# First mixer: GpSimd keeps fills and first differences, its other work goes to VectorE; 16-row triangles are inverted as 8-row blocks

## The chip, the cores and the metric

The kernel runs on one core of one Trainium2 chip. The metric is the device time of one execution in microseconds (us); the kernel before takes 2576.1 us (median of 3 runs, 2573.64 to 2580.8). In the profile PE is TensorE, PEld its weight loads, DVE is VectorE, ACT is ScalarE, POOL is GpSimd and SP the queue that issues DMAs.

## What is computed

Two decoder layers on 256 tokens of width 2048, all in float32. The first layer's mixer is RWKV-7, the second's differential attention; each is followed by a gated MLP with a short convolution, and by layer norms. The change is in the first mixer alone, whose core is a recurrence over time per head (32 heads of 64 columns):

```python
def step(S, inp):
    r_t, w_t, k_t, v_t, a_t, b_t = inp
    sa = einsum('bhij,bhj->bhi', S, a_t)
    S = S * w_t[:, :, None, :] + sa[..., None] * b_t[:, :, None, :] + v_t[..., None] * k_t[:, :, None, :]
    y = einsum('bhij,bhj->bhi', S, r_t)
    return S, y
# around it
xx = token_shift(x) - x
xr, xw, xk, xv, xa, xg = (x + xx * mu[i] for i in range(6))
r, k, v = xr @ w_rkv[0], xk @ w_rkv[1], xv @ w_rkv[2]      # and three narrow pairs for decay, a and the gate
y = group_norm(wkv7_scan(r, decay, k, v, -kk, kk * a)) + bonus
return (y * g) @ w_o
```

## The kernel before

Every weight matrix is streamed from memory in chunks of 128 x 512. `chunk` (L199 to L214) splits each 128 x 256 piece into `hi` (ScalarE, L210) and `lo` = raw - hi (L213), and `mm3` multiplies with both parts. L213 runs on VectorE, except for every `pool_every`-th piece (PACE `pool0=3` in the opening products, `pool=4` in the pipeline) and the first chunk of each opening product, which run on GpSimd. TensorE needs `hi` and `lo` of a piece before it can multiply with it.

The mixer goes through three stages. First (0 to about 150 us) the input is mixed with its shifted copy six ways (L773, then split by L191 and L192 into two parts `S`, `S1r`) beside the products for v and for the narrow pairs; the first differences `xx` are L770. Then (to about 200) the first products for r and k. Then (200 to 645) a pipeline over 8 groups of 4 heads. One step of the pipeline runs four generators beside each other, interleaved by the numbers in PACE: `chain` and `outputs` of group i (the recurrence in chunks of 64 tokens, then norm, gate and bonus), `lanes` of group i+1, `front` of group i+2 and `products` of group i+3. The last steps run `early` products with the output weights in place of the products. What the generators issue is put in one fixed order per engine, and each engine runs its list strictly in that order.

`front` (L1064) makes the scaled factors `KB` and `AR` and the 64 x 64 coupling matrices `M` (L1145), and stores M to memory (`d1`, L1153). `lanes` (L1180) inverts the unit triangular part of each M. It loads the 16 x 16 diagonal blocks back from memory (`Ml`, L1191), solves all of them row by row on VectorE (a product L1209 and a reduction L1211 for each of rows 1 to 15, over 8 right-hand columns per lane), stores the result (`d2`, L1215) and loads it as 32 x 32 blocks (`W`, L1220). Blocks of 16 are then joined to 32 (transpose L1227, 32 x 16 products L1233 and L1240) and 32 to 64 (transpose L1245, products L1251 and L1260). `W` is copied back into M (L1266 area, engines named by PACE `wc`).

On GpSimd the mixer has, per group: Lx = L - sw (L1107), the copy pc (L1114), kk times a (L1122), half of KB (L1130), r times k (L1159), fills of Ml and Tl (L1192 to L1196), KB times pc (L1198), one of the four copies of W (L1049 from `wc`), bonus times gate (L1382), and the output sum (L1388).

Of the kernel before, what the change touches and what calls it, by code (L numbers as in the profile page):

```python
# [33 lines left out]
PACE = dict(chain=37.24, front=19.56, lanes=19.55, products=40.92, pool=4, pool0=3, chain0=0, front0=0,  # L34
            lanes0=0, early0=0, products0=0, wc='PVVA', ek='AA', ez='VA', ec='AVAA', ey='V', el='V', w0=(3, 4,
# [924 lines left out]
class Groups:  # L960
# [114 lines left out]
    def front(self, g):  # L1075
# [31 lines left out]
        nc.gpsimd.tensor_tensor(out=Lx, in0=L, in1=sw, op=ALU.subtract)  # L1107
# [14 lines left out]
        nc.gpsimd.tensor_tensor(out=a, in0=kk, in1=a, op=ALU.mult)  # L1122
# [36 lines left out]
        nc.gpsimd.tensor_tensor(out=r, in0=r, in1=k, op=ALU.mult)  # L1159
# [18 lines left out]
    def lanes(self, g):  # L1178
# [15 lines left out]
        for q in range(2):
            r = slice(64 * q, 64 * q + 64)
            nc.gpsimd.memset(Tl[r].rearrange("p a b -> p (a b)")[:, 8 * q:8 * q + 7 * 17 + 1:17], 1.0)  # L1196

        nc.gpsimd.tensor_tensor(out=KB.rearrange("p c a s -> p c (a s)"), in0=KB.rearrange("p c a s -> p c (a s)"),  # L1198
# [166 lines left out]
    def outputs(self, g):  # L1365
# [98 lines left out]
```

## Time and profile before

| what | us |
|---|---|
| median of 3 runs | 2576.1 |
| the profiled execution, whole | 2568.52 |
| its span, first to last instruction | 2566.5 |
| TensorE busy in the span | 2468.5 |
| VectorE busy | 2053.8 |
| ScalarE busy | 1645.2 |
| GpSimd busy | 390.7 |

Busy shares are averages over stages. A matmul's record runs from its start to a modelled end, so that TensorE can look busy while it waits behind a piece that is not there yet. In the rows below a line number is that of the kernel before; `x` is the number of instructions, and behind the bar stand the busy time, the mean ns of one, and the idle time of the engine before them.

### The profile page before, as it was taken

How to read it: one execution, taken by the hardware profiler on the slowest of the kernel's cores; microseconds unless marked ns; L12 is line 12 of the kernel's file. 1: busy time of each engine (PE TensorE's matmuls, PEld its weight loads, DVE VectorE, ACT ScalarE, POOL GpSimd, SP SyncE). 2: the span in 40 equal slices, each digit the busy share in tenths (PEclk: the TensorE clock that was granted, in tenths of full speed). 3: DMA queues.
4: the chain of work that ended last, by engine and by line, in shares of the span. 5: the costliest groups of instructions: out<-in, count | busy, mean ns of one | idle time of the engine just before them, and what ended most of it. 6: DMA issues, size and time to landing. Idle time of an engine off the chain costs nothing.

```text
span 2566.5 us, 54810 instructions
## 1 busy us (share of the span) xinstructions
PE 2468.5 (96%) x17598; PEld 2171.5 (85%) x17598; DVE 2053.8 (80%) x5100; ACT 1645.2 (64%) x4318; POOL 390.7 (15%) x456
## 2 busy tenths in 40 slices
PE   7999989899899999999999999999999999999996
PEld 6888778767788888888889899998888888888886
DVE  8977888887897777777777877779997777777776
ACT  5765555644576666666566766666676666666664
POOL 4343344332400000000111200003300000000111
PEclk9999999999999999999999999999999999999998
DMA  6544334344466555556766555556465555566664
GB/s 191 175 129 116 102 104 108 99 121 124 125 187 192 190 190 190 190 189 184 225 190 183 156 171 171 171 167 196 145 199 188 188 188 188 188 186 185 189 190 127
DMA packets 285186, 429.63 MB, mean 167 GB/s; under 512 B 69081, under 2 KB 91617, under 8 KB 284897
## 3 DMA queue, kind: packets, MB, share of 16 engines
q1 hardware_dynamic: 284896, 426.14, 55.0%
q8 instruction: 137, 2.24, 0.4%
q14 instruction: 153, 1.25, 0.2%
HBM read 421.03 MB, written 6.57 MB: 167 GB/s over the span
## 4 chain that ended last, share of the span: by engine, by line
PE 74%; DVE 4%; ACT 1%; issue 1%; DMA 1%; POOL 0%; ACTq 0%; DVEq 0%; SPq 0%; POOLq 0%
PE psd L225 42%; PE psd L226 21%; PE psd L293 1%; PE psd L291 1%; PE psd L292 1%; DVE lo L213 1%; PE psd L897 1%; PE psd L896 1%; PE psd L898 1%; PE lnst L345 1%; PE psd L221 1%; PE psd L223 1%; PE psd L222 1%; DMA raw<-in_rw_o 0%; PE pss L656 0%
## 5 line engine op out<-in xcount | busy, mean ns | idle before, releaser
L210 ACT CAST hi<-raw 128x256 fp32r<-128x256 f32 (+1 forms) x3128 | 1231.1, 405 | 676.5 <-PE psd L225 461.2
L213 DVE TENSOR_TENSOR lo<-raw,hi 128x256 fp32r<-128x256 f32 (+1 forms) x2984 | 1287.5, 442 | 404.4 <-ACT hi L210 369.4
L225 PE MATMUL psd<-S,hi 128*128 128x512 f32 x3004 | 1056.7, 396 | 0.4 <-ACT hi L210 0.4
L226 PE MATMUL psd<-S,lo 128*128 128x256 f32 x3004 | 842.2, 280 | 4.4 <-DVE lo L213 3.8
L225 PEld LDWEIGHTS psd<-S,hi 128*128 128x128 f32 x3004 | 566.0, 188 | 132.5 <-ACT hi L210 1.2
L226 PEld LDWEIGHTS psd<-S,lo 128*128 128x128 f32 x3004 | 565.8, 188 | 5.9 <-DVE lo L213 4.5
L225 PE MATMUL psd<-hs,hi 128*128 128x512 f32 x1290 | 451.4, 394 | 0.1
L226 PE MATMUL psd<-hs,lo 128*128 128x256 f32 x1290 | 361.5, 280 | 0.0
L225 PEld LDWEIGHTS psd<-hs,hi 128*128 128x128 f32 x1290 | 241.8, 187 | 56.5 <-ACT hi L210 1.0
L226 PEld LDWEIGHTS psd<-hs,lo 128*128 128x128 f32 x1290 | 243.1, 188 | 0.4 <-DVE lo L213 0.3
L363 POOL COPY ln_acc<-X 128x256 f32<-128x256 f32 x4 | 2.1, 528 | 1230.9 <-DVE X L397 1230.9
L213 POOL TENSOR_TENSOR lo<-raw,hi 128x256 fp32r<-128x256 f32 x144 | 130.4, 913 | 301.2 <-ACT hi L210 244.1
L223 PE MATMUL psd<-S,lo 128*128 128x256 f32 x480 | 140.6, 293 | 13.8 <-DVE lo L213 8.4
L221 PE MATMUL psd<-S,hi 128*128 128x256 f32 x480 | 141.6, 295 | 0.9 <-ACT hi L210 0.5
L222 PE MATMUL psd<-S,hi 128*128 128x256 f32 x480 | 141.4, 295 | 0.0
L223 PEld LDWEIGHTS psd<-S,lo 128*128 128x128 f32 x480 | 92.8, 193 | 22.3 <-DVE lo L213 12.8
L225 PE MATMUL psd<-S1r,hi 128*128 128x512 f32 x276 | 109.9, 427 | 1.4 <-ACT o_rs L1049 0.7
L370 POOL TENSOR_TENSOR ln_acc<-ln_acc,X 128x256 f32<-128x256 f32 x49 | 40.9, 834 | 402.4 <-DVE X L409 389.1
L221 PEld LDWEIGHTS psd<-S,hi 128*128 128x128 f32 x480 | 92.5, 193 | 5.7 <-ACT hi L210 1.5
L222 PEld LDWEIGHTS psd<-S,hi 128*128 128x128 f32 x480 | 92.8, 193 | 2.9 <-issue 2.7
L221 PE MATMUL psd<-S1r,hi 128*128 128x256 f32 x284 | 87.2, 307 | 1.4 <-ACT S1r L191 0.9
L897 PE MATMUL psd<-S,lo 128*128 128x258 f32 x256 | 75.4, 295 | 10.1 <-DVE lo L213 10.1
(297 smaller groups left out, 3823.5 us busy)
## 6 DMA issues: line engine op xcount, KB each, us to landing
raw<-in_ff_up SPq DMA_DIRECT2D x676, 256.0 KB, 3.4
raw<-in_ff_down SPq DMA_DIRECT2D x320, 256.0 KB, 3.0
raw<-in_rkv SPq DMA_DIRECT2D x192, 256.0 KB, 3.5
raw<-in_da_qk SPq DMA_DIRECT2D x122, 256.0 KB, 3.4
raw<-in_da_v SPq DMA_DIRECT2D x64, 256.0 KB, 3.1
raw<-in_da_o SPq DMA_DIRECT2D x64, 256.0 KB, 3.5
raw<-in_rw_o SPq DMA_DIRECT2D x50, 256.0 KB, 3.5
raw<-in_ff_down SPq DMA_DIRECT2D x32, 192.0 KB, 2.7
```

The source lines that it names most:

```text
L210: nc.scalar.copy(out=hi[:, :s * P], in_=r)
L213: eng.tensor_tensor(out=lo[:, :s * P], in0=r, in1=hi[:, :s * P].bitcast(F32), op=ALU.subtract)
L221: nc.tensor.matmul(ps[:, :T], lhsT=hi, rhs=xs[:, :T], start=first, stop=False)
L222: nc.tensor.matmul(ps[:, :T], lhsT=hi, rhs=xs[:, T:], start=False, stop=False)
L223: nc.tensor.matmul(ps[:, :T], lhsT=lo, rhs=xs[:, :T], start=False, stop=last)
L225: nc.tensor.matmul(ps, lhsT=hi, rhs=xs, start=first, stop=False)
L226: nc.tensor.matmul(ps[:, T:], lhsT=lo, rhs=xs[:, :T], start=False, stop=last)
L291: nc.tensor.matmul(o, lhsT=xh, rhs=hi, start=k == 0 and b == 0, stop=False)
L292: nc.tensor.matmul(o, lhsT=xh, rhs=lo, start=False, stop=False)
L293: nc.tensor.matmul(o, lhsT=xl, rhs=hi, start=False, stop=k == KT - 1 and b == T // P - 1)
L370: nc.gpsimd.tensor_tensor(out=self.ln_acc[:, hs], in0=self.ln_acc[:, hs], in1=t, op=ALU.add)
L897: nc.tensor.matmul(ps[:, 2:4 + T], lhsT=lo[:, w], rhs=x[:, 2:4 + T], start=False, stop=False)
```

## The change

All lo parts of the pipeline and of the opening products go to VectorE (`pool=0`, `pool0=0`; the first chunk of each opening product stays on GpSimd), and so do the elementwise products and differences of `front`, `lanes` and `outputs`. The GpSimd copy of W goes to ScalarE (`wc='AVVA'`). GpSimd keeps the first differences, fills, the copy pc, and what other stages give it. The triangular solve stops at 8 x 8 blocks: twice as many blocks as before, spread over all 128 lanes, rows 1 to 7, each product and reduction only as wide as the row needs. A new step joins 8 to 16 with a transpose, 32 small products per group, a masked copy into the new tile Z8, and 32 more products. Z2 takes the buffer T1 that tt, T0, T1 and T2 use, one after the other.

```diff
-PACE = dict(chain=37.24, front=19.56, lanes=19.55, products=40.92, pool=4, pool0=3, chain0=0, front0=0,
-            lanes0=0, early0=0, products0=0, wc='PVVA', ek='AA', ez='VA', ec='AVAA', ey='V', el='V', w0=(3, 4,
+PACE = dict(chain=37.24, front=19.56, lanes=19.55, products=40.92, pool=0, pool0=0, chain0=0, front0=0,
+            lanes0=0, early0=0, products0=0, wc='AVVA', ek='AA', ez='VA', ec='AVAA', ey='V', el='V', w0=(3, 4,
...
-        nc.gpsimd.tensor_tensor(out=Lx, in0=L, in1=sw, op=ALU.subtract)
+        nc.vector.tensor_tensor(out=Lx, in0=L, in1=sw, op=ALU.subtract)
...
-        for q in range(2):
-            nc.sync.dma_start(out=self.dram(d2, 0, ((DBL, 64), (C, 8), (1, 16)), at=8 * C * q),
-                              in_=Tl[64 * q:64 * q + 64])
+        nc.sync.dma_start(out=self.dram(d2, 0, ((DBL // 2, P), (C, 8), (1, 8))), in_=Tl)
...
-        for i in range(1, 16):
-            nc.vector.tensor_tensor(out=tt[:, :, :i + 1], in0=Tl[:, :, :i + 1],
-                                    in1=Ml[:, 0:i + 1, i].unsqueeze(1).broadcast_to([P, 8, i + 1]), op=ALU.mult)
-            nc.vector.tensor_reduce(out=Tl[:, :, i], in_=tt[:, :, :i + 1], axis=AX.X, op=ALU.add)
+        for i in range(1, 8):
+            nc.vector.tensor_tensor(out=tt[:, :i, :i], in0=Tl[:, :i, :i],
+                                    in1=Ml[:, 0:i, i].unsqueeze(1).broadcast_to([P, i, i]), op=ALU.mult)
+            nc.vector.tensor_reduce(out=Tl[:, :i, i], in_=tt[:, :i, :i], axis=AX.X, op=ALU.add)
             if i % 3 == 0:
                 yield
...
+        T0 = g1.tile([P, 8, 32], F32, name="T1")
+        nc.vector.transpose(out=T0.rearrange("p u t -> p (u t)"), in_=W1.rearrange("p u t -> p (u t)"))
+        T0v, W1v = (x.rearrange("p u (b k i) -> p u b k i", b=2, k=2) for x in (T0, W1))
+        ps = self.pst()
+        pv = ps[:, :P].rearrange("p (u b i) -> p u b i", b=2, i=8)
+        for u in range(8):
+            for q, r in enumerate(rows):
+                be = 32 * (q % 2)
+                nc.tensor.matmul(pv[r, u], lhsT=N[q][r, u, be:be + 32], rhs=T0v[r, u, :, 0, :], start=True, stop=True)
+        nc.vector.tensor_tensor(out=self.Z8[:, :, :, 0, :], in0=pv,
+                                in1=t.x("m8", 16).rearrange("p (b i) -> p b i", b=2).unsqueeze(1).broadcast_to([P, 8, 2, 8]),
+                                op=ALU.mult)
+        yield
...
+        for u in range(8):
+            for r in rows:
+                nc.tensor.matmul(pv[r, u], lhsT=self.Z8[r, u].rearrange("p b k i -> p (b k i)"), rhs=W1v[r, u, :, 1, :],
+                                 start=True, stop=True)
+        nc.scalar.copy(out=W1v[:, :, :, 1, :], in_=pv)
+        yield
...
-        Z2 = g1.tile([P, 8, 32], F32, name="Z2")
+        Z2 = g1.tile([P, 8, 32], F32, name="T1")
```

Six more instructions change from `nc.gpsimd` to `nc.vector` in the same way: kk times a, half of KB, r times k, KB times pc, bonus times gate and the output sum.

GpSimd's list for one group, in the middle of the pipeline (`lo` is a weight part, `Tl` the tile of the solve). Before:

```order
L1388 TENSOR_TENSOR X<-o_y,bon 128x512
L1107 TENSOR_TENSOR Lx<-L,wa 128x512
L213 TENSOR_TENSOR lo<-raw,hi 128x256
L1114 COPY pc<-eL 128x8
L213 TENSOR_TENSOR lo<-raw,hi 128x256
L1122 TENSOR_TENSOR wa<-kk,wa 128x512
L1130 TENSOR_TENSOR KB<-wa 128x2x2x64 x2
L213 TENSOR_TENSOR lo<-raw,hi 128x256
L1159 TENSOR_TENSOR r<-r,k 128x512
L213 TENSOR_TENSOR lo<-raw,hi 128x256 x2
```

Now, from the opening stage to the first group:

```order
L216 TENSOR_TENSOR lo<-raw,hi 128x256
L773 TENSOR_TENSOR xx<-xz 128x256 x5
L1201 MEMSET Tl 128x64
L1202 MEMSET Tl 128x8
L989 MEMSET UV 128x1024
L994 COPY Z<-cst 32x8x16 x4
L1000 COPY Z_2562<-cst 32x8x8 x8
L1124 COPY pc<-eL 128x8
```

From there on the copy pc and the two fills of Tl are all that stands there for a group; the rest has left this list.

VectorE's list where the solve begins, behind the last join of the group before (`T` is the work tile, `bon` the bonus). Before:

```order
L1254 COPY Z_5198<-pss 32x256
L1209 TENSOR_TENSOR T_5279<-Tl,Ml 128x8x2
L1211 TENSOR_REDUCE Tl<-T_5279 128x8
L1209 TENSOR_TENSOR T_5279<-Tl,Ml 128x8x3
L1211 TENSOR_REDUCE Tl<-T_5279 128x8
L1209 TENSOR_TENSOR T_5279<-Tl,Ml 128x8x4
L1211 TENSOR_REDUCE Tl<-T_5279 128x8
```

Now:

```order
L1280 COPY T_5357<-pss 32x256
L216 TENSOR_TENSOR lo<-raw,hi 128x256
L1115 SCALAR_TENSOR_TENSOR L<-ext,wa 128x256 x2
L1215 TENSOR_TENSOR T_5438<-Tl,Ml 128x1
L1117 TENSOR_TENSOR Lx<-L,wa 128x512
L1217 TENSOR_REDUCE Tl<-T_5438 128x1
L1175 TENSOR_TENSOR bon<-pss,X 128x512
L1215 TENSOR_TENSOR T_5438<-Tl,Ml 128x2x2
L1293 COPY M<-pss 32x8x32
```

The products and reductions are shorter, other work stands between them, and the first product now stands behind the scan and a lo part.

VectorE's list at the joins (`W` is the loaded block, `Z_2562` the tile Z8). Before:

```order
L213 TENSOR_TENSOR lo<-raw,hi 128x256
L1377 SCALAR_TENSOR_TENSOR o_y<-yps,par,o_rs 128x256 x2
L1227 STREAM_TRANSPOSE T_5110<-W_4495 128x256
L1145 TENSOR_TENSOR M<-pss,ext 128x2x256 x2
L213 TENSOR_TENSOR lo<-raw,hi 128x256
```

Now:

```order
L1231 STREAM_TRANSPOSE T_5876<-W_5439 128x256
L216 TENSOR_TENSOR lo<-raw,hi 128x256
L1239 TENSOR_TENSOR Z_2562<-pss,ext 128x16x8
L216 TENSOR_TENSOR lo<-raw,hi 128x256
L1403 SCALAR_TENSOR_TENSOR o_y<-yps,par,o_rs 128x256 x2
L1408 TENSOR_TENSOR bon<-bon,o_rs 128x512
L1155 TENSOR_TENSOR M<-pss,ext 128x2x256 x2
```

The new masked copy waits for TensorE's 32 products of the new join, and only one lo part stands between it and the transpose that feeds them.

## Rows read from the trace of the kernel before

**Rows 1.** The page, part 1: busy us of each engine, share of the span, instructions
```profile
PE 2468.5 (96%) x17598; PEld 2171.5 (85%) x17598; DVE 2053.8 (80%) x5100; ACT 1645.2 (64%) x4318; POOL 390.7 (15%) x456
```

**Rows 2.** Stretches: length, busy us and instructions by engine, clock, DMA share, GB/s
```profile
37.00:150.00 113.00, 104.53 (x804) 98.96 (x803) 111.99 (x252) 79.97 (x232) 43.00 (x48) 1.00 0.57 173
200.00:645.00 445.00, 411.50 (x5016) 339.16 (x5015) 371.07 (x914) 249.88 (x607) 154.92 (x177) 0.95 0.42 111
```

**Rows 3.** The same columns, the two stretches of one group
```profile
351.00:383.00 32.00, 28.14 (x346) 23.61 (x346) 30.58 (x79) 20.15 (x50) 14.17 (x13) 0.95 0.29 89
383.00:402.00 19.00, 18.52 (x286) 16.29 (x282) 12.68 (x28) 9.72 (x23) 6.82 (x9) 1.00 0.59 129
```

**Rows 4.** Groups by shape, GpSimd, 37 to 150: busy, mean ns, idle before
```profile
L213 POOL TENSOR_TENSOR lo<-raw,hi 128x256 fp32r<-128x256 f32 x48 | 43.5, 921 | 70.6 <-ACT hi L210 55.0 <-PE psd L223 9.8 <-PE psd L222 4.1
```

**Rows 5.** Groups by shape, VectorE, 37 to 150
```profile
L773 DVE SCALAR_TENSOR_TENSOR mx<-xx,par,xz 128x256 f32<-128x256 f32 x74 | 44.7, 630 | 0.1
L213 DVE TENSOR_TENSOR lo<-raw,hi 128x256 fp32r<-128x256 f32 x95 | 43.2, 479 | 0.1
L192 DVE TENSOR_TENSOR S1r<-mx,S1r 128x256 fp32r<-128x256 f32 x62 | 28.6, 475 | 0.0
```

**Rows 6.** Groups by shape, VectorE, 770 to 1000, where GpSimd does nothing
```profile
L213 DVE TENSOR_TENSOR lo<-raw,hi 128x256 fp32r<-128x256 f32 x331 | 140.1, 424 | 46.1 <-ACT hi L210 42.3 <-PE psd L225 0.4
L526 DVE SCALAR_TENSOR_TENSOR gc<-gp,cpar,gc 128x256 f32<-128x256 f32 x41 | 19.6, 478 | 0.0
```

**Rows 7.** Timeline of VectorE: start, us, line, tiles, count
```profile
365.36 0.74 DVE L213 TENSOR_TENSOR lo<-raw,hi 128x256 fp32r<-128x256 f32 x2
...
370.43 2.38 DVE L1129 TENSOR_TENSOR KB<-k,wa 128x256 f32<-128x256 f32 x2
```

**Rows 8.** Timeline of GpSimd, same stretch
```profile
366.58 3.64 POOL L213 TENSOR_TENSOR lo<-raw,hi 128x256 fp32r<-128x256 f32 x1
```

**Rows 9.** Groups by shape, GpSimd, 351 to 383
```profile
L213 POOL TENSOR_TENSOR lo<-raw,hi 128x256 fp32r<-128x256 f32 x4 | 6.0, 1505 | 8.9 <-ACT hi L210 5.5 <-PE us L1339 3.3
L1130 POOL TENSOR_TENSOR KB<-wa 128x256 f32<-128x256 f32 x2 | 1.7, 860 | 0.1
L1122 POOL TENSOR_TENSOR wa<-kk,wa 128x512 f32<-128x512 f32 x1 | 1.5, 1476 | 0.0
...
L1107 POOL TENSOR_TENSOR Lx<-L,wa 128x512 f32<-128x512 f32 x1 | 1.3, 1269 | 1.8 <-DVE L L1105 1.8
```

**Rows 10.** Groups by shape, VectorE, 351 to 402
```profile
L213 DVE TENSOR_TENSOR lo<-raw,hi 128x256 fp32r<-128x256 f32 x24 | 10.6, 454 | 3.4 <-ACT hi L210 3.0
...
L1129 DVE TENSOR_TENSOR KB<-k,wa 128x256 f32<-128x256 f32 x2 | 2.4, 1232 | 0.0
...
L322 DVE SCALAR_TENSOR_TENSOR Lx<-Lx,o_y 128x512 f32<-128x512 f32 x1 | 1.1, 1111 | 0.0
...
L1209 DVE TENSOR_TENSOR T<-Tl,Ml 128x16 f32<-128x16 f32 x1 | 0.9, 885 | 0.0
...
L322 DVE SCALAR_TENSOR_TENSOR eL<-eL,t 128x512 f32<-128x512 f32 x1 | 0.7, 670 | 0.0
...
L1209 DVE TENSOR_TENSOR T<-Tl,Ml 128x24 f32<-128x24 f32 x1 | 0.2, 185 | 0.0
...
L1211 DVE TENSOR_REDUCE Tl<-T 128x8 f32<-128x16 f32 x1 | 0.2, 172 | 0.0
```

**Rows 11.** Groups by line, VectorE, 0 to 760: the triangular inversion
```profile
L1209 DVE TENSOR_TENSOR T<-Tl,Ml 128x16 f32<-128x16 f32 (+14 forms) x120 | 42.0, 350 | 3.9 <-POOL Ml L1192 1.7
...
L1211 DVE TENSOR_REDUCE Tl<-T 128x8 f32<-128x16 f32 (+14 forms) x120 | 27.1, 226 | 2.5
```

**Rows 12.** Groups by shape, TensorE, 0 to 760
```profile
L1233 PE MATMUL pss<-T,M 32*32 32x16 f32 x512 | 5.8, 180 | 0.3 <-DVE R L1049 0.3
```

**Rows 13.** DMA issues, 0 to 760: count, KB each, median us to landing
```profile
W<-d SPq DMA_DIRECT2D x32, 32.0 KB, 2.1
d<-Tl SPq DMA_DIRECT2D x16, 32.0 KB, 3.2
```

More of the change, by code (lines that the diff above doesn't have):

```diff
@@ L80, in _const_layout @@
     base = n
-    for name, w in (("bd1", P), ("cent", P), ("mask", P), ("reset", T)):
+    for name, w in (("bd1", P), ("cent", P), ("mask", P), ("reset", T), ("m8", 16)):
         at[name] = n
@@ L109, in _constants @@
     put("mask", np.concatenate([s < t, s <= t], 1).astype(np.float32))
+    m8 = np.ones((P, 16), np.float32)
+    m8[np.arange(P) % 32 >= 24, :8] = 0
+    put("m8", m8)
     reset = np.ones((P, T), np.float32)
@@ L991, in open @@
             nc.gpsimd.tensor_copy(out=self.Z[r, :, 16:], in_=t.cst[r, o:o + 16].unsqueeze(1).broadcast_to([32, 8, 16]))
+        self.Z8 = fx.tile([P, 8, 2, 2, 8], F32, name="Z8")
+        for q in range(4):
+            r = slice(32 * q, 32 * q + 32)
+            for b in range(2):
+                o = CCOL["ident"] + 32 * q + 16 * b + 8
+                nc.gpsimd.tensor_copy(out=self.Z8[r, :, b, 1, :],
+                                      in_=t.cst[r, o:o + 8].unsqueeze(1).broadcast_to([32, 8, 8]))
         self.d2 = d2p.tile([P, DBL * 64 // P], F32, name="d2")
@@ L1120, in front @@
                                     op0=ALU.subtract, op1=ALU.mult)
-        nc.gpsimd.tensor_tensor(out=a, in0=kk, in1=a, op=ALU.mult)
+        nc.vector.tensor_tensor(out=a, in0=kk, in1=a, op=ALU.mult)
         nc.vector.scalar_tensor_tensor(out=k, in0=t1, scalar=1.0, in1=k, op0=ALU.add, op1=ALU.mult)
@@ L1129, in front @@
             nc.vector.tensor_tensor(out=self.half(KB[:, :, par, :], par), in0=k_, in1=e_, op=ALU.mult)
-            nc.gpsimd.tensor_tensor(out=self.half(KB[:, :, 1 - par, :], par), in0=a_, in1=e_, op=ALU.mult)
+            nc.vector.tensor_tensor(out=self.half(KB[:, :, 1 - par, :], par), in0=a_, in1=e_, op=ALU.mult)
         nc.vector.scalar_tensor_tensor(out=AR[:, :, 0, :], in0=c3, scalar=-1.0, in1=_ch(_fl(Lx)), op0=ALU.mult,
@@ L1157, in front @@
             yield from self.gates(g + 1)
-        nc.gpsimd.tensor_tensor(out=r, in0=r, in1=k, op=ALU.mult)
+        nc.vector.tensor_tensor(out=r, in0=r, in1=k, op=ALU.mult)
         for jj, j in js:
@@ L1183, in lanes @@
         KBT = s["KBT"] = self.g2.tile([P, GT * NC, P], F32, name="KBT")
-        Ml = g1.tile([P, 16, 16], F32, name="Ml")
-        Tl = g1.tile([P, 8, 16], F32, name="Tl")
+        Ml = g1.tile([P, 8, 8], F32, name="Ml")
+        Tl = g1.tile([P, 8, 8], F32, name="Tl")
         tt = g1.tile([P, 8, 32], F32, name="T1")
@@ L1188, in lanes @@
         Z = self.Z
-        for q in range(2):
-            nc.sync.dma_start(out=Ml[64 * q:64 * q + 64], in_=self.dram(d1, 0, ((DBL, 64), (C, 16), (1, 16))))
-        nc.gpsimd.memset(Ml.rearrange("p a b -> p (a b)")[:, 0:256:17], 1.0)
+        nc.sync.dma_start(out=Ml, in_=self.dram(d1, 0, ((DBL // 2, P), (C, 8), (1, 8))))
         nc.gpsimd.memset(Tl, 0.0)
[L1194 to L1198, printed above, removed]
+        nc.gpsimd.memset(Tl.rearrange("p a b -> p (a b)")[:, 0:64:9], 1.0)
+        nc.vector.tensor_tensor(out=KB.rearrange("p c a s -> p c (a s)"), in0=KB.rearrange("p c a s -> p c (a s)"),
                                 in1=pc.rearrange("p j c o -> p (j c) o").broadcast_to([P, GT * NC, 2 * C]),
@@ L1381, in outputs @@
         nc.tensor.matmul(ps, lhsT=t.x("bd1"), rhs=_fl(y2), start=True, stop=True)
-        nc.gpsimd.tensor_tensor(out=bon, in0=bon, in1=rs, op=ALU.mult)
+        nc.vector.tensor_tensor(out=bon, in0=bon, in1=rs, op=ALU.mult)
         nc.vector.tensor_scalar(out=_fl(y2), in0=ps, scalar1=1.0 / 64, scalar2=GN_EPS, op0=ALU.mult, op1=ALU.add)
@@ L1387, in outputs @@
         nc.vector.tensor_tensor(out=y, in0=y, in1=rs, op=ALU.mult)
-        nc.gpsimd.tensor_tensor(out=self.V[:, j0:j0 + GT, :], in0=y, in1=bon, op=ALU.add)
+        nc.vector.tensor_tensor(out=self.V[:, j0:j0 + GT, :], in0=y, in1=bon, op=ALU.add)
         if g >= NG - 3:
```

3 lines of the change are left out of this document (2 added, 1 removed).

## Prediction, written before the change was run

> **What bounds the kernel now.** I read the page's busy shares first, then the stretches, then groups of instructions by shape, and last the timelines of VectorE and GpSimd beside each other. Over the whole span TensorE is busy 96% and GpSimd 15% [rows 1], which says nothing about the change, since the change is in the first 650 us. By stretch, two places have another limit than TensorE. From 37 to 150 us VectorE is busy 111.99 of 113 us [rows 2], with TensorE at 104.53. In the pipeline (200 to 645) VectorE has 371.07 of 445 us, but not evenly: one group takes 51 us, of which VectorE is busy in 30.58 of the first 32 and in 12.68 of the next 19, while TensorE has 28.14 and 18.52 [rows 3]. So the first part of a group goes at VectorE's speed and the second, at 97%, at TensorE's. The group behind it has the same two parts. ScalarE is at 20.15 and 9.72 and sets nothing.
>
> **What GpSimd costs VectorE.** A lo part takes VectorE 424 ns on average where GpSimd does nothing [rows 6], 479 from 37 to 150 [rows 5], and 454 within a group [rows 10]. Two products for KB took 2.38 us [rows 7], 1232 ns each [rows 10], while GpSimd worked on its own half; a lo part of the same shape and input count is 424. GpSimd pays too: one of its lo parts lasted 3.64 us behind VectorE's list [rows 8], against a mean of 921 in [rows 4]. The two engines get in each other's way when both read from SBUF.
>
> Sum for 37 to 150, from [rows 5] less the undisturbed 478 and 424 of [rows 6]: 74 x (630 - 478) = 11.2, 95 x (479 - 424) = 5.2, 62 x (475 - 424) = 3.2, in all 19.6 us that VectorE gets back, if no work of GpSimd is left there (the first differences end before 37 us). What comes in: the 48 lo parts [rows 4]. Two lo parts back to back take 0.74 us [rows 7], so one more costs 0.74 - 0.42 = 0.32, taken as 0.34: 16.3 us. Net -3.3; I take -3. Ends: -8.5 (TensorE's idle time there, 113 - 104.5, all gone) and +3 (the 48 parts at their full 424 ns, 20.4 us, with a seventh of the disturbance staying).
>
> **One group of the pipeline, first part (32 us).** Disturbance that goes, from [rows 10]: lo parts 24 x (454 - 424) = 0.7; KB 2 x (1232 - 424) = 1.6; the second Lx step 1111 against 670 for its twin eL, 0.4; the first product of the solve 885 against 185 for the next larger one, 0.7. Sum 3.4 us.
>
> The solve: 42.0 + 27.1 = 69.1 us over 8 groups [rows 11], 8.6 per group. The seven products and reductions that replace it are as wide as 1 to 49 elements; I price each pair as the smallest of the old ones, 185 + 172 ns [rows 10], so 2.5 us. By the line's means (350 and 226) it would be 4.0. Saved 6.1; 4.6 at the other end.
>
> What VectorE takes over in this part: four 512-wide instructions (Lx and kk times a in [rows 9], and two of the same shape, the output sum and r times k), at the 670 ns of an undisturbed 512-wide one [rows 10] 2.7 us; two products for KB at 0.42, 0.8; four lo parts [rows 9] at 0.34, 1.4. Sum 4.9.
>
> Net -3.4 - 6.1 + 4.9 = -4.6 of 32 us. TensorE is busy 28.14 us of it; if all of that were work, only 3.9 could be gained. I take 3.9. Part of what counts as busy there may be records that wait in TensorE's queue, so 3.9 is no hard floor.
>
> **Second part (19 us).** VectorE gets the bonus product (0.67), KB times pc (twice as wide, 1.34), four lo parts (1.4), a transpose and the masked copy: 4 us and some onto 12.68, which fits under 19. TensorE gets two more rounds of small products like L1233, whose 512 records take 5.8 us over 8 groups [rows 12]: 0.72 each, 1.45 per group. Since TensorE sets this part, that is paid: +1.45. The copy of W that ScalarE takes over lies under its idle half. SP issues one load and one store of the blocks per group where it issued two of each; no gain is counted for it. The output sum of a group gets shorter on VectorE, which only the last group can feel, under 1 us, counted at nothing.
>
> **An added wait.** Three instructions on VectorE now stop its list: the first product of the solve waits for TensorE to be done with the shared buffer T1, the first transpose for the loaded W, the masked copy for TensorE's new products. Behind them are lo parts, and TensorE waits for those. Store and load of the blocks take 3.2 and 2.1 us [rows 13]. In the new list about a dozen instructions (lo parts, two M, r times k) stand between last reduction and first transpose, some 5 us, and VectorE has 6.3 us idle in that part. So I cost the stops at nothing; other end 4.5 us per group (2 for the load, 1.5 for the new products behind a transpose, 1 for T1).
>
> **Sum.** Per group -3.9 + 1.45 = -2.45, times 8 = -19.6; with the -3 of the opening, -22.6. The profiled execution took 2568.5 us (span 2566.5, 2.0 around it), so 2545.9, and by the ratio of the median to it (2576.1 / 2568.5) **2553.5 us**, 0.9% less.
>
> **A rule weighed.** The rows on KB and lo parts show mutual delay by amounts between 30 and 800 ns. The Trainium skill, "SBUF — State Buffer", section "Who interferes with whom", says that a VectorE instruction with two SBUF inputs and a GpSimd instruction that reads SBUF exclude each other, the later one standing still for the whole of the other. By it each GpSimd product would cost VectorE up to its whole length; the trace agrees where KB took 1232 ns, and not in the 24 lo parts. What that makes of the time is the last rival.
>
> **Rivals.**
> *TensorE takes it back.* The 28.14 us of TensorE in the first part are work, its own round trips in the recurrence set the pace, and the part gives only the 1.45 that the new products cost. Then -3 is left: 2573. For it: TensorE is at 88% there. Against: VectorE is idle under 1.5 us of 32.
> *The stops decide (slower).* The three stops hold VectorE's list for 4.5 us per group in the part that TensorE sets, and the lo parts behind them come late. Then -3.9 + 1.45 + 4.5 = +2.05, times 8 = +16.4, less 3: +13.4, 2589. It decides from 2.45 us per group on. For it: only one lo part stands between the new transpose and the masked copy. Against: the list moves the same kinds of stops that are there now, and VectorE has 6.3 us free there.
> *More than the sum.* GpSimd's 14.17 busy us in the first part [rows 3] cost VectorE most of their length, in copies and pieces I have not priced, and TensorE's 28.14 us are largely waiting. Then the part loses 8 instead of 3.9: (-8 + 1.45) x 8 = -52, and -8.5 in the opening: 2515. Against: the lo parts of [rows 10], 24 of them, lose 30 ns on average, not 700.
>
> **Chances and range.** Forecast 0.67 (own range 2532 to 2568), TensorE takes it back 0.13, stops 0.12, more than the sum 0.08. About 0.3%, 8 us, is what a measurement of this kernel can tell from no change. Faster by more: 0.67 + 0.08 = 0.75; within: 0.13; slower: 0.12. The 80% range leaves out most of the stops and the lower half of the last rival: 2522 to 2580. The low end also holds a group at -4.6 with the opening at -8.5.
>
> **What would show it.** Right: from 37 to 150 lo parts at about 424 ns on VectorE, the stretch a few us shorter; the period of a group down from 51 to about 48.5; the solve near 2.5 us per group; GpSimd under 10 us in the pipeline. Wrong: VectorE waiting at the masked copy or the first transpose by more than 2 us per group; TensorE's waits for lo parts longer than before; the period unchanged with VectorE idle in the first part, which would say that the recurrence's round trips set it.

## The result: faster, and the profile after

The changed kernel takes 2540.2 us (median of 4 runs, 2539.45 to 2543.21), the kernel before on the same chip 2576.8 (4 runs, 2573.64 to 2580.8): ratio 0.9859, 95% interval 0.9838 to 0.988. The forecast was 2553.5, its 80% range 2522 to 2580. The profiled execution has a span of 2537.5 us against 2566.5, which is 29.0 less.

The page's first part: busy us of each engine, share of the span, instructions. It answers to [rows 1].

```profile
PE 2461.7 (97%) x18622; PEld 2170.2 (86%) x18622; DVE 2030.6 (80%) x5192; ACT 1648.8 (65%) x4334; POOL 172.0 (7%) x236
```

GpSimd has lost more than half of its time. TensorE's busy time is hardly less, over a shorter span. Next, two stretches of the changed kernel (length, busy us and instructions by engine, clock, DMA share, GB/s), against [rows 2]:

```profile
37.00:150.00 113.00, 108.88 (x853) 104.54 (x852) 111.17 (x316) 85.21 (x246) 0.27 (x2) 1.00 0.59 176
200.00:645.00 445.00, 423.19 (x6112) 352.18 (x6113) 371.30 (x972) 264.88 (x655) 12.91 (x34) 0.98 0.42 113
```

VectorE is as busy from 37 to 150 us as before, with 316 instructions in place of 252. From 200 to 645 it has the same 371 us, while TensorE went from 411.50 to 423.19 and its granted clock from 0.95 to 0.98. One group, with the columns of [rows 3]:

```profile
329.00:359.00 30.00, 28.89 (x378) 24.29 (x378) 28.39 (x80) 21.84 (x52) 0.68 (x3) 1.00 0.33 89
359.00:377.00 18.00, 17.91 (x382) 16.01 (x382) 13.04 (x30) 8.89 (x24) 0.00 (x0) 1.00 0.59 140
```

The two parts are 30 and 18 us long where they were 32 and 19, and the clock in the first is 1.00 where it was 0.95. Groups of VectorE's instructions by shape (busy us, mean ns | idle before), first from 37 to 150 us against [rows 5], then in the group from 329 to 377 against [rows 10]:

```profile
L216 DVE TENSOR_TENSOR lo<-raw,hi 128x256 fp32r<-128x256 f32 x153 | 58.3, 416 | 1.0 <-ACT hi L213 0.9
L776 DVE SCALAR_TENSOR_TENSOR mx<-xx,par,xz 128x256 f32<-128x256 f32 x77 | 35.1, 477 | 0.0
L195 DVE TENSOR_TENSOR S1r<-mx,S1r 128x256 fp32r<-128x256 f32 x62 | 25.3, 417 | 0.3
```

```profile
L216 DVE TENSOR_TENSOR lo<-raw,hi 128x256 fp32r<-128x256 f32 x33 | 13.3, 419 | 4.3 <-ACT hi L213 3.9 <-PE us L1365 0.3
...
L1139 DVE TENSOR_TENSOR KB<-k,wa 128x256 f32<-128x256 f32 x2 | 0.8, 418 | 0.0
```

These durations are now within 8 ns of those of [rows 6]. The triangles, by line, 0 to 760 us, against [rows 11]; and TensorE's two added rounds, against [rows 12]:

```profile
L1215 DVE TENSOR_TENSOR T<-Tl,Ml 128x1 f32<-128x1 f32 (+6 forms) x56 | 10.6, 190 | 0.7
...
L1217 DVE TENSOR_REDUCE Tl<-T 128x1 f32<-128x1 f32 (+6 forms) x56 | 9.5, 170 | 0.9
```

```profile
L1247 PE MATMUL pss<-W,Z 32*32 32x16 f32 x512 | 6.2, 180 | 1.1 <-DVE M L1155 0.9
...
L1238 PE MATMUL pss<-T,M 32*32 32x16 f32 x512 | 5.8, 180 | 0.1
```

So the solve went from 69.1 to 20.1 us in all, and the added rounds take 12.0 us.

To see where the 29 us came from I take four marks in both traces: the first copy of r out of PSUM (the opening ends there), the first output o_y that VectorE writes, the fifth, and the end.

| stretch | before | after | difference |
|---|---|---|---|
| start to first r | 156.3 | 149.3 | -7.0 |
| first r to first o_y (the pipeline fills) | 131.1 | 121.4 | -9.8 |
| first to fifth o_y (four periods) | 205.3 | 192.6 | -12.7 |
| fifth o_y to the end | 2073.8 | 2074.3 | +0.5 |

The period of a steady group is 51.3 us before and 48.15 after. What I had not weighed shows in the clock column (the share of full speed that TensorE was granted) of three stretches, first of the kernel before, then of the changed one:

```profile
150.00:280.00 130.00, 119.91 (x1112) 106.83 (x1114) 98.65 (x226) 73.19 (x175) 50.90 (x60) 0.91 0.42 115
280.00:480.00 200.00, 182.62 (x2469) 156.37 (x2465) 173.80 (x416) 119.05 (x283) 79.45 (x87) 0.97 0.39 102
480.00:650.00 170.00, 161.05 (x1809) 123.28 (x1810) 136.38 (x352) 86.62 (x223) 46.86 (x57) 0.94 0.43 119
```

```profile
150.00:280.00 130.00, 123.25 (x1534) 109.88 (x1535) 102.88 (x260) 76.67 (x185) 5.39 (x20) 0.99 0.48 128
280.00:480.00 200.00, 192.61 (x3174) 164.91 (x3172) 174.11 (x450) 131.53 (x314) 2.63 (x12) 1.00 0.40 104
480.00:650.00 170.00, 157.51 (x1822) 123.10 (x1820) 137.68 (x366) 91.07 (x238) 12.26 (x22) 0.97 0.42 120
```

The trace's own records of the granted clock put TensorE at 1.2 instead of 2.4 GHz for 58.0 us of the time from 150 to 650 us before, and for 13.7 us after.

### The profile page after: what moved, and what is told of

The parts are those of the page before. It is cut to its first block, busy times and chain, and to the rows that moved or that the text cites. A ratio compares the mean times of both kernels' runs of the same rounds, so it can differ in the third digit from the quotient of the medians.

```text
span 2537.5 us, 56569 instructions
## 1 busy us (share of the span) xinstructions
PE 2461.7 (97%) x18622; PEld 2170.2 (86%) x18622; DVE 2030.6 (80%) x5192; ACT 1648.8 (65%) x4334; POOL 172.0 (7%) x236
## 4 chain that ended last, share of the span: by engine, by line
PE 81%; DVE 3%; ACT 1%; DMA 1%; issue 1%; SPq 0%; POOL 0%; ACTq 0%; DVEq 0%; POOLq 0%
PE psd L228 43%; PE psd L229 22%; PE psd L224 2%; PE psd L225 2%; PE psd L226 2%; PE psd L296 1%; PE psd L295 1%; PE psd L294 1%; PE psd L900 1%; PE psd L899 1%; PE psd L901 1%; DVE lo L216 1%; DMA raw<-in_rw_o 1%; PE lnst L348 1%; PE pss L1152 0%
## 5 line engine op out<-in xcount | busy, mean ns | idle before, releaser
L216 DVE TENSOR_TENSOR lo<-raw,hi 128x256 fp32r<-128x256 f32 (+1 forms) x3124 | 1308.3, 430 | 418.9 <-ACT hi L213 375.9
L224 PE MATMUL psd<-S,hi 128*128 128x256 f32 x480 | 138.5, 289 | 1.6 <-ACT hi L213 1.4
L225 PE MATMUL psd<-S,hi 128*128 128x256 f32 x480 | 137.6, 287 | 0.0
L228 PE MATMUL psd<-S1a,hi 128*128 128x512 f32 x240 | 84.9, 398 | 0.0
L229 PE MATMUL psd<-S1r,lo 128*128 128x256 f32 x276 | 80.8, 293 | 1.5 <-DVE lo L216 1.5
```

Of the source, the lines that this page charges most:

```text
L216: eng.tensor_tensor(out=lo[:, :s * P], in0=r, in1=hi[:, :s * P].bitcast(F32), op=ALU.subtract)
L224: nc.tensor.matmul(ps[:, :T], lhsT=hi, rhs=xs[:, :T], start=first, stop=False)
L225: nc.tensor.matmul(ps[:, :T], lhsT=hi, rhs=xs[:, T:], start=False, stop=False)
L228: nc.tensor.matmul(ps, lhsT=hi, rhs=xs, start=first, stop=False)
L229: nc.tensor.matmul(ps[:, T:], lhsT=lo, rhs=xs[:, :T], start=False, stop=last)
```

## Experiments

The change has three parts that can be set one by one: S, the solve in blocks of eight rows (with its join); P, the products (and a copy of W) taken from GpSimd; L, the lo parts taken from GpSimd. All eight combinations have a time. (In the profile lines `S` and `L` are tiles.) Each ratio is against the kernel before on the same chip, with its 95% interval. "Low clock" is the time at 1.2 GHz from 150 to 650 us by the trace's clock records, "period" a quarter of the time from first to fifth o_y. These columns come from one profiled execution of each kernel; that of L took 2546.4 us where its median is 2553.9, and had the highest clock of its six.

| kernel | ratio | interval | first r, us | period, us | low clock, us |
|---|---|---|---|---|---|
| before | 1 | | 156.3 | 51.3 | 58.0 |
| S | 0.9981 | 0.9966 to 0.9996 | 158.6 | 51.7 | 37.5 |
| P | 0.9926 | 0.9903 to 0.9949 | 157.5 | 51.6 | 47.8 |
| L | 0.9925 | 0.9906 to 0.9944 | 147.2 | 51.8 | 30.7 |
| S and P | 0.9913 | 0.9886 to 0.994 | 158.3 | 48.1 | 13.7 |
| S and L | 0.9937 | 0.9913 to 0.9961 | 148.4 | 50.2 | 20.5 |
| P and L | 0.9887 | 0.9869 to 0.9905 | 149.2 | 49.65 | 51.2 |
| all three | 0.9859 | 0.9838 to 0.988 | 149.3 | 48.15 | 13.7 |

My theory at first was the prediction's own: VectorE's time sets the first part of a group, so the shorter solve brings the gain and the moved work costs. Rival A: the moves bring it. Rival B: the solve brings all of it.

**P and L without S.** Edit to the kernel before: GpSimd's products, copies and lo parts to VectorE, the solve as it was.

```
-pool=4, pool0=3, ... wc='PVVA'
+pool=0, pool0=0, ... wc='AVVA'
-nc.gpsimd.tensor_tensor(out=Lx, ...)      (and six more products)
+nc.vector.tensor_tensor(out=Lx, ...)
```

> The kernel before with all of GpSimd's moves and the 16-row solve kept. Theory (what GpSimd reads disturbs VectorE, and a piece costs VectorE less than the disturbance): the opening stage to 150 us gains 6 us as in the changed kernel; in a group VectorE loses 3.4 us of disturbance and takes 4.9 us over in its full part, so groups get 1 us longer to 1 us shorter; in all 0 to -14 us, ratio 0.9945 to 1.000. Rival A (the moves alone make the gain, since GpSimd's results came late): -29 us, ratio about 0.987. Rival B (the solve makes it all, and the moves cost): +10 us, 1.004.

Measured 2544.67 us, 0.9887 (0.9869 to 0.9905): rival A.

**S alone.** The changed kernel with all that undone.

```
-pool=0, pool0=0, ... wc='AVVA'
+pool=4, pool0=3, ... wc='PVVA'
-nc.vector.tensor_tensor(out=Lx, ...)      (and six more products)
+nc.gpsimd.tensor_tensor(out=Lx, ...)
```

> The changed kernel with GpSimd's work put back (products, a quarter of the weight parts, one copy of W) and the 8-row solve kept. Theory: nothing in the opening; per group 6.1 us less on VectorE and 1.45 us more on TensorE, some 3 us of 51: -20 to -28 us, ratio 0.989 to 0.992. Rival A: -5 us or less, ratio above 0.997. Rival B: -36 us, 0.986.

Measured 2567.65 us, 0.9981: about 5 us where I expected 20 to 28, rival A again. Its stretch 280 to 480 us:

```profile
280.00:480.00 200.00, 186.33 (x2936) 158.24 (x2928) 154.86 (x358) 116.61 (x280) 72.29 (x78) 0.96 0.38 99
```

VectorE is busy 154.86 of 200 us, against 173.80 in the kernel before, and the period did not move. The saved time is now idle time of VectorE, so VectorE's busy time was not what set the period while GpSimd had the products. What the others waited for in that stretch (us in total, times, longest), first GpSimd, then ScalarE:

```profile
POOL lo L216 <- ACT hi L213: 67.2, 17, 5.8
```

```profile
ACT r L1171 <- POOL r L1169: 11.2, 3, 3.9
```

GpSimd stands a third of the time at lo parts that wait for ScalarE's rounded part, with the products queued behind, and ScalarE waits for a product. The kernel before has 68.1 us of the first wait and 7.6 of the second, so these are not new. That they bound S alone is how I read it, and not shown; taking the products away as well (S and P, below) shortens its period by 3.6 us, taking the lo parts (S and L) by 1.5.

**L in the opening alone.** Edit to the kernel before:

```
-pool0=3
+pool0=0
```

> The kernel before with pool0=0 alone: in the opening products every weight part but the first chunk's is made on VectorE. Theory: the opening to 150 us ends 5 to 7 us earlier and this stays to the end: ratio 0.9972 to 0.998. Rival (the opening is TensorE's or the DMAs', and the 6 us come from elsewhere): no change, 0.999 to 1.001.

Measured 2561.9 us, 0.9959 (0.9944 to 0.9975), some 10 us where the theory had 5 to 7. The first copy of r comes at 148.3 us, 7.9 earlier, and the end of the trace 5.4 earlier.

**L, everywhere.** Edit to the kernel before:

```
-pool=4, pool0=3
+pool=0, pool0=0
```

> The kernel before with pool0=0 and pool=0: all weight parts on VectorE, the products of front, lanes and outputs stay on GpSimd. Theory: the opening's 6 us; in a group eight parts at 0.34 us come in (2.7 us) and 0.7 to 2 us of disturbance go, half of it in the part that VectorE fills, so 0 to +0.7 us per group: -6 to 0 us, ratio 0.9977 to 1.000. Rival A (late parts from GpSimd held TensorE): -15 us or more, 0.994.

Measured 2553.88 us, 0.9925, as rival A had it (15 us or more), not the theory (0 to 6). The steady period stays at 51.8 in the trace.

**P alone.** Edit to the kernel before: the products and the copy of W, not the lo parts.

```
-wc='PVVA'
+wc='AVVA'
-nc.gpsimd.tensor_tensor(out=Lx, ...)      (and six more products)
+nc.vector.tensor_tensor(out=Lx, ...)
```

> The kernel before with the products (and the copy of W) taken from GpSimd alone: lo parts stay where they were, one in four on GpSimd, and the solve keeps its 16 rows. Theory L (GpSimd's products are slow results on the way of a group, so that its latency sets the period until they move): the period of a group falls by about 2 us from 51.3, the opening stays, about -9 to -14 us, ratio 0.9945 to 0.9965. Rival C (what counts is VectorE's time, lost to GpSimd's reading; any piece of GpSimd's work costs it alike): the products add their own 4.9 us a group to VectorE and the lo parts still disturb it, so no gain, ratio 0.998 to 1.003.

Measured 2551.81 us, 0.9926: the gain is more than theory L's, but the period, which that theory had falling, stays at 51.6; why is taken up below. The gain lies before the first o_y (-9) and after the fifth (-7.5 us to the end).

**S and P.** Edit to the changed kernel:

```
-pool=0, pool0=0
+pool=4, pool0=3
```

> The changed kernel with one lo part in four put back on GpSimd: solve of 8 rows and products on VectorE. Theory L: with the products gone the shorter solve counts, so it takes about 1.5 us a group more than the products alone give; period near 48 to 48.5, ratio 0.989 to 0.9925, short of the whole change by the opening and the filling steps. Rival C: the lo parts on GpSimd still hold VectorE up, ratio 0.995 to 0.998.

Measured 2548.79 us, 0.9913, with a period of 48.1, as theory L had it. So S alone and P alone leave the period, and together they give all of it. Not all of that reaches the end: behind the fifth o_y the trace of S and P takes 2073.6 us, that of P 2066.3.

**S and L.** Edit to the changed kernel: the products and the copy of W back on GpSimd.

```
-nc.vector.tensor_tensor(out=Lx, ...)      (and six more products)
+nc.gpsimd.tensor_tensor(out=Lx, ...)
```

> The changed kernel with the products (and the copy of W) put back on GpSimd: solve of 8 rows, and all lo parts on VectorE. Theory L: the products' latency still sets the period, so the solve gives nothing on top of the lo parts moved alone (0.9925): ratio 0.991 to 0.994, period 51 to 52. Rival C: without lo parts on GpSimd VectorE has less disturbance and is the bound, so its 6 us a group from the solve count in part: ratio 0.987 to 0.9895, period 49 to 50.

Measured 2554.27 us, 0.9937, as theory L had it, but with a period of 50.2, between its 51 to 52 and rival C's 49 to 50.

**Why P alone does not shorten the period.** One group of P alone in slices of 4 us, the columns as above:

```profile
340.00:344.00 4.00, 2.69 (x43) 2.03 (x44) 3.89 (x9) 2.79 (x7) 0.13 (x1) 0.91 0.44 91
344.00:348.00 4.00, 4.00 (x31) 3.65 (x27) 3.07 (x12) 2.48 (x4) 0.00 (x0) 0.50 0.12 35
348.00:352.00 4.00, 4.00 (x39) 2.09 (x39) 0.99 (x2) 1.43 (x6) 0.72 (x1) 0.50 0.00 0
352.00:356.00 4.00, 4.00 (x19) 2.63 (x20) 2.35 (x7) 2.37 (x8) 0.00 (x0) 0.81 0.23 71
```

From 344 us TensorE has work all the time (4.00 of 4) and does it at 0.50 of its clock for some 10 us, in each of the four groups from 280 to 480. The stretch as a whole, first of P alone, then of S and P:

```profile
280.00:480.00 200.00, 193.79 (x2451) 162.08 (x2450) 169.61 (x444) 119.96 (x284) 34.22 (x51) 0.89 0.38 102
```

```profile
280.00:480.00 200.00, 192.10 (x3193) 165.78 (x3192) 166.63 (x415) 128.59 (x307) 31.61 (x45) 1.00 0.40 108
```

Clock 0.89 against 1.00. The kernel before has 0.97 there: so P alone has three times its time at the low level, and may have given back through the clock what it had won. If so, TensorE needs no shorter solve there, only something to do. The next edit adds useless products to P alone:

```
 ps = self.pst()
 pv = ps[:, :P].rearrange("p (u t) -> p u t", t=16)
+nc.tensor.matmul(ps[:, T:], lhsT=t.c("ident"), rhs=t.cst[:, :T], start=True, stop=True)
 for u in range(8):
```

and the same ahead of the second and third round.

> The kernel with only the products moved (16-row solve, lo parts as before; 0.9926 of before; in each steady group TensorE's granted clock falls to 0.5 for about 10 us, 47.8 us in all from 150 to 650) with a useless 128x256 product of TensorE added ahead of the first, second and third round of the joins, about 0.5 us each, 1.6 us a group. Theory K (the clock that TensorE is granted is part of the gain: it falls after TensorE has gone short of work around the joins, and TensorE then works through its queue at half speed): the added work keeps it busy, the time at the low clock falls below 25 us and the period from 51.6 towards 49.5, ratio 0.985 to 0.990, so more work is faster. Rival N (the low clock only goes with the waiting and sets nothing): the added work costs nothing up to its length, 0 to 12.7 us, ratio 0.9926 to 0.9975.

Measured 2543.58 us, 0.989 (0.9869 to 0.9911), as theory K had it: added work made it 8.2 us faster than P alone, by the medians. The two kernels ran on different chips, where the kernel before took 2569.5 and 2571.0. The runs don't overlap (2539.52 to 2546.73 against 2549.91 to 2554.35), the two intervals do by 0.0008. The stretch 280 to 480, and the added products (busy us, mean ns):

```profile
280.00:480.00 200.00, 196.27 (x2709) 166.70 (x2708) 183.15 (x474) 129.31 (x304) 39.35 (x56) 1.00 0.42 111
```

```profile
L1251 PE MATMUL pss<-cst 128*128 128x256 f32 x16 | 5.9, 441 | 0.1
...
L1230 PE MATMUL pss<-cst 128*128 128x256 f32 x16 | 4.9, 385 | 0.2 <-DVE M L1145 0.2
L1239 PE MATMUL pss<-cst 128*128 128x256 f32 x16 | 4.8, 381 | 0.0
```

The clock is 1.00 and the period 47.8 us, 3.8 less than without them, though the products themselves are 15.6 us over 8 groups, 1.95 each. The low clock from 150 to 650 us is 10.2 us where it was 47.8. In P it had taken 10.2 us in three of the four groups and 13.7 in the first. At half the rate 10.2 us hold 5.1 us of work; less 1.95 for the products it leaves 3.2, and up to 5.1 if they lie in holes. The Trainium skill, "TensorE: Matmul & The Clock Gate", section "Terms", prices time at the low clock the same way: at half of it is half of that time lost. The run agrees where TensorE is the bound. That it isn't always, S shows: clock 0.96 from 280 to 480 against 0.89 in P, and the same period. Of the 15.9 us that the trace with the products has gained on P's by the fifth o_y, 6.9 are lost again by the end; what takes them is not known.

The other executions bear the clock out. Over the whole span it is 0.981 to 0.987 in the six runs of P and 0.988 to 0.993 in the five with the products. Of the 43 runs of the kernel before that stand beside the experiments, the nine with the lowest clock (0.979 and less) have a median of 2579.4 us, the nine with the highest (0.984 and more) 2564.9.

The trace of P and L shows it within one execution, with the 16-row solve. Its four groups, from o_y to o_y:

```profile
273.00:324.10 51.10, 48.65 (x629) 42.06 (x630) 45.25 (x125) 30.45 (x73) 0.79 (x5) 0.93 0.39 104
324.10:370.70 46.60, 45.02 (x628) 39.44 (x628) 43.50 (x121) 30.71 (x73) 0.97 (x5) 0.96 0.43 114
370.70:418.00 47.30, 45.73 (x632) 39.85 (x628) 43.75 (x123) 31.02 (x73) 1.05 (x5) 0.96 0.44 113
418.00:471.60 53.60, 49.51 (x630) 42.32 (x628) 43.86 (x122) 30.70 (x73) 0.96 (x5) 0.87 0.37 98
```

The period goes with the clock, from 46.6 us at 0.96 to 53.6 at 0.87, over nearly the same instructions. In the last group TensorE is busy 4.5 us longer than in the second, near half of the 10.2 us that it spends more at the low clock, and idle 2.5 us longer. So periods below the changed kernel's 48.15 need no shorter solve: two of these four have them.

With two products at each place:

```
+nc.tensor.matmul(ps[:, T:], lhsT=t.c("ident"), rhs=t.cst[:, :T], start=True, stop=True)
+nc.tensor.matmul(ps[:, T:], lhsT=t.c("ident"), rhs=t.cst[:, :T], start=True, stop=True)
```

> As the run with one useless product ahead of three rounds of the joins, with two ahead of each: about 1 us each place, 3.2 us a group. Theory K: the low clock goes at least as far, but the products are longer than the holes: ratio 0.986 to 0.993. Rival N: 0 to 25 us slower than the products alone, ratio 0.994 to 1.002.

Measured 2556.96 us, 0.9941 (0.9918 to 0.9964), in rival N's range and just above theory K's. By itself this run would speak against K. In its trace two of the groups fell to the low clock again, for 6.8 us each, with periods of 51.7 and 52.1, and two did not, with 49.3 and 49.2. Over the whole span its clock, 0.988 to 0.993, is as high as with one product. So the second products gained nothing in clock, and the 13.4 us that the kernel is slower are near their length, 15.6 us by the first ones' time.

**What GpSimd's work costs when nobody needs it.** Edit to the changed kernel, at every second weight part of the pipeline:

```
+nc.gpsimd.tensor_copy(out=self.scr[:, :1], in_=r[:, :1])
+nc.gpsimd.tensor_tensor(out=self.scr[:, :T], in0=self.cst, in1=self.cst, op=ALU.subtract)
```

> The changed kernel with, at every second weight part of the pipeline, a GpSimd copy of one column of the loaded weight and a 128x256 difference of two constants that nobody waits for: some 16 a group of about 0.9 us each, so GpSimd works about as long as in the kernel before, reading from SBUF, with no result on anybody's way. Theory L (GpSimd's cost was its late results): ratio 0.986 to 0.988, lo parts of VectorE at most 30 ns longer on average. Rival C (GpSimd's reading takes VectorE's time, as the prediction's terms for the disturbance have it, or by more): at least 3 us a group back, ratio 0.993 to 0.998.

Measured 2559.38 us, 0.9955 (0.9937 to 0.9972): 0.0096 of the time, some 25 us, lost again to results that nobody waits for. Theory L is wrong in this, rival C right. (The added copy reads a loaded weight, so it could hold up the next load; from 200 to 480 us the loads wait for it 3.9 us in all.) GpSimd's groups from 200 to 480 us:

```profile
L217 POOL TENSOR_TENSOR scr<-cst 128x256 f32<-128x256 f32 x92 | 68.3, 743 | 7.4
L216 POOL COPY scr<-raw 128x1 f32<-128x1 f32 x91 | 34.6, 380 | 167.1 <-DMA raw<-in_rkv 165.3
```

VectorE's lo parts in the same stretch: the kernel before, the changed one, and this one.

```profile
L213 DVE TENSOR_TENSOR lo<-raw,hi 128x256 fp32r<-128x256 f32 x137 | 66.2, 497 | 14.7 <-ACT hi L210 13.6
```

```profile
L216 DVE TENSOR_TENSOR lo<-raw,hi 128x256 fp32r<-128x256 f32 x194 | 77.9, 419 | 24.8 <-ACT hi L213 22.9 <-PE us L1365 1.5
```

```profile
L219 DVE TENSOR_TENSOR lo<-raw,hi 128x256 fp32r<-128x256 f32 x186 | 86.5, 486 | 18.8 <-ACT hi L213 17.0 <-PE us L1371 0.8
```

The next view of the same lo parts, in the same order, gives the shortest, the median and the longest in ns:

```profile
L213 DVE TENSOR_TENSOR lo<-raw,hi x137: 401/420/1972, 200.1 to 479.6; 128x256 fp32r<-128x256 f32 x137
```

```profile
L216 DVE TENSOR_TENSOR lo<-raw,hi x194: 379/418/427, 199.8 to 479.5; 128x256 fp32r<-128x256 f32 x194
```

```profile
L219 DVE TENSOR_TENSOR lo<-raw,hi x186: 379/423/871, 203.2 to 479.5; 128x256 fp32r<-128x256 f32 x186
```

The medians agree; the means differ by a few very long ones, 20 of 137 over 460 ns before (mean 955), 40 of 186 here (mean 732), none of the changed kernel's. The Trainium skill, "SBUF — State Buffer", section "Who interferes with whom", has the later of the two engines stand still for the whole of the other's instruction. The longest here, 871 ns, is a lo part and 450 ns more; it began 22 ns behind one of GpSimd's differences, of 612 ns, as that rule would have it for one that is hit. But most are not hit, and 102.9 us of GpSimd's work took 186 x 67 ns = 12.5 us from the lo parts. Beside that TensorE's low clock is up from 13.7 to 30.7 us, and the period is 51.2. How the 25 us divide between the two, the run doesn't tell.

**The added join.** The changed kernel without joining blocks of 8 to blocks of 16 rows; that part of the inverse is left out.

```
-T0 = g1.tile([P, 8, 32], F32, name="T1")
-nc.vector.transpose(...)                  (and all up to the copy)
-nc.scalar.copy(out=W1v[:, :, :, 1, :], in_=pv)
```

> The changed kernel without the added join of blocks of 8 to blocks of 16 rows (a transpose, two rounds of 64 small products, a masked copy and a copy of ScalarE a group); that part of the inverse is left out. The prediction had the two rounds at 1.45 us a group on the path, 11.6 us in all, and the stops at nothing: ratio 0.981 to 0.983 against the changed kernel's 0.9859. Rival T (TensorE has holes in which the small products lie, so they cost less than their length): ratio 0.9845 to 0.987. Rival S (the stops behind the join cost too): below 0.980.

Measured 2523.36 us, 0.982 (0.9795 to 0.9845). The period is 46.9, 1.25 less, though unevenly: two of the four groups take 45.8 us, two 48.0, as in the changed kernel. The whole is 0.0039 or 10 us less than the changed kernel, with intervals that overlap by 0.0007. The forecast's 1.45 a group fits, though the interval just reaches rival T's low end too.

The run answers one more question. The added join's small products could be what keeps the clock up in the changed kernel, as the useless ones do. They are not needed for it, since the clock holds without them:

```profile
280.00:480.00 200.00, 198.27 (x2621) 168.14 (x2622) 177.06 (x455) 134.69 (x322) 2.42 (x12) 1.00 0.39 106
```

**One more move.** The changed kernel with the layer norm's centring on VectorE:

```
-nc.gpsimd.tensor_tensor(out=self.X[:, j, :], in0=self.X[:, j, :], in1=self.ln_dm, op=ALU.subtract)
+nc.vector.tensor_tensor(out=self.X[:, j, :], in0=self.X[:, j, :], in1=self.ln_dm, op=ALU.subtract)
```

> The changed kernel with the layer norm's centring, too, on VectorE where GpSimd has it. A candidate that may beat it. If late results of GpSimd cost there as they did in the mixer: 2 to 8 us less, ratio 0.983 to 0.985; if the centring lies under TensorE's work: the same time, 0.985 to 0.987; if VectorE's list is what the norm waits for: above 0.988.

Measured 2533.26 us, 0.9857 (0.9833 to 0.9882). This cannot be told from the changed kernel.

## Why the prediction was right, and where its reasons were not

*The opening, -3.* Measured -7.0 at the first r, -7.9 with that edit alone. The mechanism was right, GpSimd's parts gone and VectorE at 416, 477 and 417 ns; the term that came back was forecast at 19.6 us and is 74 x 153 + 95 x 63 + 62 x 58 = 20.9 by the means of [rows 5]. What was measured is near the low end that I gave, -8.5; how the other 2 to 3 us divide, the runs don't tell. (The high end, +3, is +3.6 by the numbers beside it: 20.4 less six sevenths of 19.6.)

*The first part of a group, -3.4 - 6.1 + 4.9, cut at 3.9.* This step failed, although the size came out. The solve fell by (69.1 - 20.1) / 8 = 6.1 us a group, exactly as priced, and by itself it brought 5 us in all. Averaged over the four pairs of the table that differ in S alone, it is worth 0.0012, 3 us; P is worth 0.0065, 17 us, and L 0.0053, 14 us. By the eight intervals an estimate for each average is 0.0014 to either side, so S cannot be told from nothing, and P and L can. I had the moves at a cost of 1.5 us a group in the first part. That the period came out near 48.5 is in part luck: a gain put on the solve is about the size of one that the moves bring. Two reasons:
1. Disturbance was taken too small. I priced 24 lo parts of one group at 454 ns; over 200 to 480 us the mean of 137 is 497. That group was a mild one. With all of GpSimd's work moved to it and the old solve, VectorE is busy 44.1 us a steady group (176.36 in the four of P and L), before it was 44.3: the moves cost it nothing, where my terms had 1.5 us for the first part and 3.4 for the second.
2. TensorE's time was taken as fixed. I read 0.95 in the clock column of [rows 2] and [rows 3] and did not ask what it cost. A place where it fell, in the kernel before, shows how GpSimd came into it. GpSimd's timeline (start, us, line, tiles), then TensorE's:

```profile
179.12 2.66 POOL L1122 TENSOR_TENSOR wa<-kk,wa 128x512 f32<-128x512 f32 x1 [0.95 <-DVE t L1119]
181.86 1.66 POOL L1130 TENSOR_TENSOR KB<-wa 128x256 f32<-128x256 f32 x2
183.49 1.17 POOL L213 TENSOR_TENSOR lo<-raw,hi 128x256 fp32r<-128x256 f32 x1
```

```profile
182.12 0.38 PE L223 MATMUL psd<-S,lo 128*128 128x256 f32 x1 [0.60 <-DVE lo L213]
...
182.70 0.28 PE L221 MATMUL psd<-S,hi 128*128 128x256 f32 x1
182.81 0.28 PE L222 MATMUL psd<-S,hi 128*128 128x256 f32 x1
184.71 0.58 PE L223 MATMUL psd<-S,lo 128*128 128x256 f32 x1 [1.62 <-POOL lo L213]
185.09 0.41 PE L221 MATMUL psd<-S,hi 128*128 128x256 f32 x1
185.30 0.41 PE L222 MATMUL psd<-S,hi 128*128 128x256 f32 x1
```

The lo part at 183.49 stands on GpSimd behind a product of 2.66 us and two of 0.8. TensorE waits 0.60 us for a lo part of VectorE and 1.62 us for this one. The record of the clock goes to the low level at 184.3, within that wait. Then its products last 0.41 us, not 0.28, and start every 0.21 us, not every 0.12. In this stretch, 150 to 280 us, the clock is 0.91 before and 0.99 after; filling is 9.8 us shorter. It is shorter by 10.3 in P and 9.5 in L too, each with the clock at 0.99 there, by 7.3 in P and L, 3.0 in S and L and 1.7 in S alone, each with 0.96.

In the steady groups the runs fit one account, in which not every link was tested: P takes the period's first bound away, the clock takes that back, and S, or useless products, keep the clock up. The first link is argued: the one steady group of the kernel before without any low clock still takes 50.3 us, those of P with useless products 47 to 49. The part on the clock is shown by the added products and by the groups of P and L. That S in the changed kernel acts by the same way, and not through VectorE's time as well, is argued from S and P: the low clock from 280 to 480 is gone there too, and its period, 48.1, is no shorter than that of P with useless products and the old solve, 47.8.

*The second part, +1.45.* Right in size: 1.25 by the run without the join, as the mean of uneven groups.

*The stops at nothing.* Right. The changed kernel's waits of VectorE, 200 to 645 us (us in total, times, longest):

```profile
DVE lo L216 <- ACT hi L213: 38.8, 72, 2.3
...
DVE T L1271 <- ACT W L1059: 1.4, 1, 1.4
...
DVE T L1280 <- ACT T L1279: 1.1, 1, 1.1
```

The masked copy, the added transpose and the first product of the solve don't appear among them. The rival with the stops is out. So is TensorE taking all of it back, as a rival about the whole time; as a mechanism it was there, in P alone.

*The period, 48.5.* Measured 48.15. The four unsteady groups were given 9.8 us in the sum; the fill alone gave 9.8, and the end of the mixer nothing. So the total of the four was met by a place that the sum did not single out.

*The total.* Forecast -22.6 against the profiled execution, measured -29.0. (The last product of the sum is 2553.4, not 2553.5.) Of the 13.3 us between 2553.5 and 2540.2, 6.4 are terms of the sum, the opening (4.0) and the steady periods (2.9) above all. The other 7 lie in how the two profiled executions stand to their medians: 2568.5 is 8.3 under the median of the runs before beside it, 2540.27 is at that of the runs after.

*Open:* what exactly lets the clock fall. The length of a wait alone is not it: it fell with waits of 0.60 and 1.62 us here, and in P at 394.5 and 445.7 us with waits of 0.6 and 0.7; the changed kernel waits up to 0.9 us from 280 to 480 without a fall, and P with useless products 1.4 us at 286.6. And whether P and L with a few useless products would beat the changed kernel: P with them has a shorter period (47.8) and keeps the old solve. It wasn't run.

## What to carry to other kernels

Read the clock column of each stretch before you share out TensorE's time: a stretch under 1.00 with TensorE busy is time that may come back, and TensorE's busy time there is not a floor. When two engines share a bottleneck, test parts of a change singly and in pairs; here neither part alone moved the period, and both together did. Price a helper engine by the long tail of what it does to its neighbour over many groups, not by one group's mean.

## What was not expected of the hardware

- Three added 128x256 products of TensorE a group, 1.95 us, made the group 3.8 us shorter (51.6 to 47.8), with the granted clock at 1.00 in place of 0.89. In the whole kernel 8.2 us were left of that.
- GpSimd's work that nobody waits for costs some 25 us of 2540, for 102.9 us of it in 200 to 480 us; the median lo part of VectorE is 423 ns against 418, the longest 871 against 427.
